# Nine raw weight buffers, x times rstd on GpSimd chunk by chunk, the modulated x in PSUM, spills on ScalarE's queue and residual x fetched ahead, in a one-core hybrid RG-LRU / pooling block

## The chip, the cores and the metric

The kernel runs on one core of one Trainium2 chip. The metric is the device time of one execution in microseconds (us); the times given are medians of repeated runs on the chip. The engines are called PE (TensorE; PEld are its weight loads), DVE (VectorE), ACT (ScalarE), POOL (GpSimd) and SP (SyncE, which here only issues DMAs).

## The reference, cut to what matters

256 latent and 256 context tokens of width 4096 pass one mixer layer, all in fp32:

```python
mod = silu(c) @ w_ada + b_ada                 # shift, scale, gate: 3 x 4096
h  = rmsnorm(x, g_norm) * (1 + scale) + shift
xa, xb, ga, gb = split(h @ w_in)              # 4 x 4096
xa_c = (modulated rmsnorm(ctx)) @ w_in[:, :4096]
ya = rglru_branch(xa, xa_c, ...)              # conv, two gates per head and direction, scans
yb = pool_branch(xb, w_pool, ...)             # windows 2, 4, 8, 16
mixed = concat(ya * silu(ga), yb * silu(gb))
out = rmsnorm(x + gate * (mixed @ w_out), g_final)
```

Shift, scale and gate come from the weights `w_ada` (a product with one vector for the latent and one for the context tokens), so `w_ada` is read in full, as `w_in` and `w_out` are.

## The kernel before

Everything is held transposed: a tile has 128 features as partitions and the 512 tokens (latent, then context) along the free dimension. fp32 products are made from splits: each operand is `hi`, rounded to fp32r, plus the rest `lo`. A unit of weights is a 128x1024 tile of 512 KB that SP loads into a buffer `raw` (pool of RAWB = 6); ACT casts it to `hi` (pool of 4, L97) and `lo = raw - hi` is made (pool of 3, L99), by POOL for the xa projection and by DVE elsewhere.

The stages:

- **Start.** x and ctx (32 tiles) come in, their squares are summed over the features (L402, L403) and L412 sums over partitions; `rstd_of` (L160) makes the reciprocal root. Meanwhile PE makes the first chunk's shift and scale rows from `w_ss` units (L237). `to_cols` and `finish_mod` (L202 to L204) turn rows into the columns `colA`, `colB`.
- **xa.** The 32 feature tiles of h are dealt in nine chunks of 2, 2, 4, 4, ... tiles (CHUNKS). `prep_h(k)` multiplies x tile k by rstd (L300, on DVE), applies colA and colB (L303, on ACT, in place) and splits the result into `hhi` and `hlo` (L130, L131). `xa_units(c)` then multiplies chunk c with its part of `w_in`, three matmuls to a product (L337 to L339), and adds the partial sum into 32 accumulators: three of four output tiles through ACT and POOL (L345, L346), the fourth on DVE (L348). Beside chunk c the shift and scale of chunk c + 1 are made out of `w_ss` units: a few on PE (L237; SHARES says how many), most on DVE, as multiply-adds into two PSUM tiles (L211 to L219). `softplus` (L358), a chain of some 25 small DVE operations on the scan's decay, stands after chunk 1.
- **Mixer.** The latent projections and pooling products (two matmuls to a product, L566 with 512 and L567 with 256 columns), beside them the recurrent heads.
- **Output.** `make_mix` splits the gated branches; 16 blocks of two output tiles, 16 units each, are multiplied with `w_out`. Beside them DVE sums three groups of `w_gate` units (L213; the first group came earlier). `out_evac` folds a tile, multiplies by gate, adds the residual x, squares it for the final norm and, for the first ten blocks, spills y to DRAM.
- **End.** The spilled tiles are read back, the final norm's rstd is made, and y is scaled and stored.

The order is written by `run(events)`: events of kind "w" (a weight unit that is split) and "a" (a raw unit that is used as it is) are loaded LOOK = 4 and LOOK_A = 2 events of their kind ahead; "s" events are other work. `spread` deals side work evenly among main work. All buffers of `raw` serve both kinds and are handed out in the order of the loads. A scheduler then fixes the order of each engine at build time, taking an instruction that its model finds ready before an earlier one that it finds waiting. All DMAs are issued by SP, in order. PSUM holds four tiles of 512 columns (`mm_tile`) and two of 1024 (`wide_tile`).

Of the kernel before, what the change touches and what calls it, by code (L numbers as in the profile page):

```python
# [7 lines left out]
F32 = mybir.dt.float32  # L8
F32R = mybir.dt.float32r
AF = mybir.ActivationFunctionType  # L10
ALU = mybir.AluOpType
ADD, SUB, MUL = ALU.add, ALU.subtract, ALU.mult

P = 128
D = 4096
KT = D // P
T = 256
# [4 lines left out]
GATE3 = (0.08, 0.7)  # L22
GATE_FROM, GATE_END = 0.9, 0.99
SPILL_Y = 10
EPS = 1e-6
POOL_ADDS = 3
EARLY = 4
NPREP = 3
LAGS = (0, 2, 5, 7, 10)
LRU_SPAN = 91  # L30
RAWB, HIB, LOB = 6, 4, 3
LOOK = 4
LOOK_A = 2
X_STEP = 3
SHARES = (16, 4, 11, 3, 0, 0, 0, 0, 0, 0, 0, 0)
CHUNKS = (2, 2, 4, 4, 4, 4, 4, 4, 4)
# [10 lines left out]


def spread(main, side, lo=0.0, hi=1.0):
    """Places the entries of side evenly among those of main, from the fraction lo of main to hi."""  # L50
    out, done, n = [], 0, len(main)
    a, b = lo * n, hi * n
    for i, m in enumerate(main):
        out.append(m)
        want = min(len(side), max(0, int((i + 1 - a) / (b - a) * len(side) + 1e-9)))
        while done < want:
            out.append(side[done])
            done += 1
    return out + side[done:]
# [3 lines left out]
def block_kernel(ctx, tc, xc, cvec, vecs, consts, w_ss, w_gate, w_xa, w_lat, w_pool, w_rec, w_out, out):  # L63
# [16 lines left out]
    def temp(name, dt=F32):  # L80
        return tpool.tile([P, 512], dt, name=name, tag="t")

    def mm_tile():
        return ps_mm.tile([P, 512], F32, name="mm", tag="mm")
# [9 lines left out]
    def load_w(src, eng=None):  # L94
        raw = load_raw(src)
        hi = hip.tile([P, W], F32R, name="hi", tag="hi")
        act.copy(out=hi, in_=raw)  # L97
        lo = lop.tile([P, W], F32R, name="lo", tag="lo")
        (eng or dve).tensor_tensor(out=lo, in0=raw, in1=hi.bitcast(F32), op=SUB)  # L99
        return hi, lo  # L100

    def run(events):
        queues = {}
# [22 lines left out]
    def S_(f):  # L126
        return ("s", f)

    def split(hi, lo, src):
        act.copy(out=hi, in_=src)  # L130
        dve.tensor_tensor(out=lo, in0=src, in1=hi.bitcast(F32), op=SUB)  # L131

# [1 line left out]
    cst = cpool.tile([P, 276], F32, name="cst")  # L134
    nc.sync.dma_start(out=cst, in_=consts)
    ident = cst[:, 0:4]
# [20 lines left out]
    dve.tensor_tensor(out=sc6[:, :, 2:4], in0=sc, in1=sig, op=MUL)  # L157
    act.activation(out=sig, in_=sig, func=AF.Sqrt)

    def rstd_of(ps, r, v, s):  # L160
        """Leaves -2 * rsqrt(ps / D + EPS) in r: one Newton step after the square root."""
        dve.tensor_scalar(out=v, in0=ps, scalar1=1.0 / D, scalar2=EPS, op0=MUL, op1=ADD)
        act.activation(out=s, in_=v, func=AF.Sqrt)
        dve.reciprocal(out=r, in_=s)
        dve.tensor_tensor(out=v, in0=v, in1=r, op=MUL)
        dve.tensor_tensor(out=v, in0=v, in1=r, op=MUL)
        dve.scalar_tensor_tensor(out=r, in0=v, scalar=-3.0, in1=r, op0=ADD, op1=MUL)

# [1 line left out]
    colA = cpool.tile([P, KT, 2], F32, name="colA")  # L170
    colB = cpool.tile([P, KT, 2], F32, name="colB")
    gate = cpool.tile([P, KT], F32, name="gate")
# [116 lines left out]
            to_cols(st["rb"], 2, 512, dst)  # L289
        return [unit(k) for k in range(KT)], S_(rows), S_(cols)  # L290

# [1 line left out]
    hT = [None] * KT  # L293
    hc = [None] * KT

    def prep_h(k):
        def f():
            x = xt[k]
            if k >= CHUNKS[0]:
                dve.tensor_tensor(out=x, in0=x, in1=rstd, op=MUL)  # L300
            for v in range(2):
                xs = x[:, v * T:(v + 1) * T]
                act.activation(out=xs, in_=xs, func=AF.Identity, scale=colA[:, k, v:v + 1], bias=colB[:, k, v:v + 1])  # L303
            hi, lo = temp("hhi", F32R), temp("hlo", F32R)
            split(hi, lo, x)
            hc[k] = (hi, lo)
        return S_(f)

# [7 lines left out]
            hc[k] = None  # L316
        return S_(f)

# [1 line left out]
    acc = [None] * 32  # L320
    xa_sp = [None] * (2 * KEEP) + [dram.tile([P, 512], F32, name=f"xa_sp{o}") for o in range(2 * KEEP, 32)]
    ya_sp = [dram.tile([P, 512], F32, name=f"ya_sp{h}") for h in range(HEADS)]
# [1 line left out]
    def xa_units(c):  # L324
        k0, n = chunk_kt[c]
        per = W // n // P

        def unit(i):
            def f(w):
                hi, lo = (t.rearrange("p (k m) -> p k m", k=n) for t in w)  # L330
                for j in range(per):
                    o = i * per + j
                    ps = mm_tile()
                    for k in range(n):
                        a, b = hc[k0 + k]
                        wh, wl = hi[:, k, j * P:(j + 1) * P], lo[:, k, j * P:(j + 1) * P]
                        pe.matmul(out=ps, lhsT=wh, rhs=a, start=(k == 0), stop=False)  # L337
                        pe.matmul(out=ps, lhsT=wh, rhs=b, start=False, stop=False)  # L338
                        pe.matmul(out=ps, lhsT=wl, rhs=a, start=False, stop=(k == n - 1))  # L339
                    if c == 0:  # L340
                        acc[o] = slot("acc")
                        act.copy(out=acc[o], in_=ps)
                    elif c < NC - 1 and o % 4 < POOL_ADDS:
                        part = temp("part")
                        act.copy(out=part, in_=ps)  # L345
                        nc.gpsimd.tensor_tensor(out=acc[o], in0=acc[o], in1=part, op=ADD)  # L346
                    else:
                        dve.tensor_tensor(out=acc[o], in0=ps, in1=acc[o], op=ADD)  # L348
                    if c == NC - 1 and o >= 2 * KEEP:
                        nc.sync.dma_start(out=xa_sp[o], in_=acc[o])  # L350
                        acc[o] = None
            return W_(w_xa[xa_base[c] + i], f, nc.gpsimd)
        return [unit(i) for i in range(32 // per)]
# [25 lines left out]

    ada = [ada_units(c) for c in range(NC)] + [([],)]  # L380

# [1 line left out]
    xt = []  # L383
    first = ada[0][0] + list(ada[0][1:])

# [25 lines left out]
    stat = mm_tile()  # L411
    pe.matmul(out=stat, lhsT=ones, rhs=ssq, start=True, stop=True)  # L412
    rstd = slot("rstd")
    rstd_of(stat, rstd, temp("v"), temp("s"))
    for k in range(CHUNKS[0]):
        dve.tensor_tensor(out=xt[k], in0=xt[k], in1=rstd, op=MUL)
    while first:
        first_unit()
    events = [prep_h(k) for k in range(CHUNKS[0])]
# [1 line left out]
    for c in range(NC):  # L421
        main = xa_units(c)
        if c + 1 < NC:
            k1, n1 = chunk_kt[c + 1]
            preps = [prep_h(k) for k in range(k1, k1 + n1)]
            au, ar, ac = ada[c + 1]
            au = au[early:]
            nxt = ada[c + 2][0]
            cut = len(nxt) // EARLY
            lag = [nxt[cut * LAGS[i] // 10:cut * LAGS[i + 1] // 10] for i in range(4)]  # L430
            keeps = [keep_h(k) for k in range(chunk_kt[c][0], k1)]
            events += spread(main, au + lag[0] + [ar] + lag[1] + [ac] + lag[2] + preps[:NPREP] + lag[3]) + keeps + preps[NPREP:]
            early = cut
        else:
            events += main + [keep_h(k) for k in range(chunk_kt[c][0], KT)]
        if c == 1:
            events.append(S_(softplus))

# [1 line left out]
    def lru_pieces(h):  # L440
        st = {}

# [94 lines left out]
            return [sigm(d, 0), sigm(d, 1), expo(d), root(d), scan(d, 0), scan(d, 1)]  # L537
        return [conv(0), conv(1)], [gates(0)] + post(0) + [gates(1)], post(1)

# [1 line left out]
    def fold(ps, dst):  # L541
        tmp = temp("fold")
        act.copy(out=tmp[:, 0:T], in_=ps[:, T:T2])
# [122 lines left out]
    both = spread(both, gu, GATE_FROM, GATE_END)  # L666
    events += both[:-4] + [gr] + both[-4:-1] + [gc] + both[-1:]

# [1 line left out]
    mix = [None] * 64  # L670

    def make_mix(n):
# [12 lines left out]
    def out_evac(blk):  # L685
        def f(j, ps):
            ct = 2 * blk + j
            if j == 0:
                xr = temp("xr")
                nc.sync.dma_start(out=xr.rearrange("p (k t) -> p k t", k=2),  # L690
                                  in_=xc[ct:ct + 2, :, 0:T].rearrange("k p t -> p k t"))
                ys.append(xr)
            y = ys[blk][:, j * T:(j + 1) * T]
            v = temp("ov")[:, 0:T]
            fold(ps, v)
            dve.scalar_tensor_tensor(out=y, in0=v, scalar=gate[:, ct:ct + 1], in1=y, op0=MUL, op1=ADD)
            if ct == 0:
                sums["s"] = temp("ssum")[:, 0:T]
                act.activation(out=sums["s"], in_=y, func=AF.Square)
            else:  # L700
                act.activation(out=v, in_=y, func=AF.Square)
                if ct < 30:
                    dve.tensor_tensor(out=sums["s"], in0=sums["s"], in1=v, op=ADD)
                else:
                    sums[ct] = v
            act.activation(out=y, in_=y, func=AF.Identity, scale=gf[:, ct:ct + 1])
            if j == 1 and blk < SPILL_Y:
                nc.sync.dma_start(out=y_sp[blk], in_=ys[blk])
        return f

    def warm_sqrt():
        t = temp("warm")[:, 0:1]
        act.activation(out=t, in_=ones[:, 0:1], func=AF.Sqrt)

    events += [make_mix(n) for n in range(4)] + [S_(warm_sqrt)]
    main = [block_units([w_out[blk, i] for i in range(16)], mix, out_evac(blk)) for blk in range(16)]
    pair = [u for two in zip(main[0], main[1]) for u in two]
    main = spread(pair, [make_mix(n) for n in range(4, 32)], 0.0, 28 / 32) + [u for m in main[2:] for u in m]
    side, held = [], []
# [14 lines left out]
    for i, part in enumerate((sums["s"], sums[30], sums[31])):  # L734
        pe.matmul(out=stat[:, 0:T], lhsT=ones, rhs=part, start=(i == 0), stop=(i == 2))
    rf = temp("rf")[:, 0:T]
    rstd_of(stat[:, 0:T], rf, temp("v")[:, 0:T], temp("s")[:, 0:T])
    for blk in range(16):
        y = ys[blk].rearrange("p (k t) -> p k t", k=2)
        dve.tensor_tensor(out=y, in0=y, in1=rf.unsqueeze(1).broadcast_to([P, 2, T]), op=MUL)  # L740
# [76 lines left out]
```

## Time and profile before

| | |
|---|---|
| median of 3 runs | 2993.46 us (2992.93 to 2996.02) |
| profiled execution, first to last instruction | 2998.8 us, 5.3 us above the median; no other time is given for this execution |
| mean granted PE clock | 0.991 |
| busy | PE 97%, PEld 80%, DVE 75%, ACT 52%, POOL 18% |
| read from and written to HBM | 661.6 MB and 15.2 MB, 226 GB/s over the span |

The busy time of an engine is the time covered by its instructions. Matmuls overlap in the records (one begins before the one ahead of it has ended), and one that waits for its operands between two others can be hidden in that overlap, so what PE loses in a stretch is read from the count of its instructions there and their pitch at full pace, and not from its busy share alone. The rows of the trace name an instruction by its line, engine, operation and tiles; in square brackets or behind a bar is how long its engine sat idle before it and what ended the wait. A line can be that of a helper: L99 is every `lo`, L91 every load into `raw`.

### The profile page before, as it was taken

What the parts mean: (1) busy time and instruction counts of PE and PEld (TensorE: products, weight loads), DVE (VectorE), ACT (ScalarE), POOL (GpSimd) and SP (SyncE); (2) the same over time, 40 slices, a digit from 0 to 9 for tenths busy, and PEclk for the clock granted to TensorE, in tenths of its full rate; (3) what the DMA queues carried; (4) which work ended last, traced back from release to release, by engine and by line L of the source; (5) the groups of instructions that cost most, each with busy time, mean ns of one, the idle gap of its engine ahead of it and who ended that gap; (6) DMA issues with size and microseconds to landing.
All of it is one profiled execution on the core that took longest, in us unless ns stands there. A gap on an engine that the chain in (4) does not pass through costs nothing.

```text
span 2998.8 us, 40342 instructions
## 1 busy us (share of the span) xinstructions
PE 2909.6 (97%) x14992; PEld 2405.3 (80%) x14992; DVE 2256.7 (75%) x2661; ACT 1559.9 (52%) x2112; POOL 530.7 (18%) x304
## 2 busy tenths in 40 slices
PE   5999999999999999999999999999999999999997
PEld 2656777778788888888888888888888888878886
DVE  6999999998447788888777777778888766665444
ACT  4442344434436666677666666666464443333442
POOL 1466777777520000000000000000000000000000
PEclk9999999999999999999999999999999999999998
DMA  8777787887365555565665566667978888786665
GB/s 301 279 261 252 262 263 261 272 277 250 126 183 176 176 177 175 179 183 172 186 185 181 185 188 189 196 195 251 326 232 318 318 288 286 264 279 216 193 191 171
DMA packets 201142, 679.47 MB, mean 227 GB/s; under 512 B 22000, under 2 KB 30320, under 8 KB 200944
## 3 DMA queue, kind: packets, MB, share of 16 engines
q1 hardware_dynamic: 200944, 676.89, 68.9%
q8 instruction: 117, 1.92, 0.3%
q14 instruction: 81, 0.66, 0.1%
HBM read 661.60 MB, written 15.20 MB: 226 GB/s over the span
## 4 chain that ended last, share of the span: by engine, by line
PE 84%; DVE 6%; DMA 6%; issue 1%; POOL 1%; ACT 1%; SPq 0%; DVEq 0%; POOLq 0%; ACTq 0%
PE mm L566 38%; PE mm L567 19%; PE mm L337 6%; PE mm L338 6%; PE mm L339 6%; DMA raw<-in_w_gate 4%; DVE wide L213 3%; PE wide L478 2%; PE wide L480 2%; PE wide L479 2%; PE mm L237 2%; DMA raw<-in_w_ss 1%; DMA x<-in_xc 1%; DVE lo L99 1%; DVE hlo L131 1%
## 5 line engine op out<-in xcount | busy, mean ns | idle before, releaser
L97 ACT CAST hi<-raw 128x1024 fp32r<-128x1024 f32 x832 | 871.9, 1049 | 968.6 <-PE mm L566 576.3
L99 DVE TENSOR_TENSOR lo<-raw,hi 128x1024 fp32r<-128x1024 f32 x704 | 856.5, 1221 | 371.5 <-PE mm L567 282.7
L566 PE MATMUL mm<-hT,hi 128*128 128x512 f32 x3072 | 1086.8, 399 | 0.0
L567 PE MATMUL mm<-hT,lo 128*128 128x256 f32 x3072 | 862.7, 281 | 0.0
L213 DVE SCALAR_TENSOR_TENSOR wide<-raw,sc,wide 128x1024 f32<-128x1024 f32 (+1 forms) x556 | 662.4, 1240 | 153.5 <-DMA raw<-in_w_gate 119.6
L566 PE MATMUL mm<-mix,hi 128*128 128x512 f32 x2048 | 724.7, 398 | 0.0
L566 PEld LDWEIGHTS mm<-hT,hi 128*128 128x128 f32 x3072 | 577.2, 188 | 144.5 <-ACT mix L130 0.9
L567 PE MATMUL mm<-mix,lo 128*128 128x256 f32 x2048 | 577.4, 282 | 15.3 <-DVE lo L99 15.1
L567 PEld LDWEIGHTS mm<-hT,lo 128*128 128x128 f32 x3072 | 580.2, 189 | 1.3
L566 PEld LDWEIGHTS mm<-mix,hi 128*128 128x128 f32 x2048 | 386.0, 188 | 95.1 <-ACT hi L97 1.7
L337 PE MATMUL mm<-hhi,hi 128*128 128x512 f32 x1024 | 404.1, 396 | 13.1 <-ACT hhi L130 10.7
L338 PE MATMUL mm<-hlo,hi 128*128 128x512 f32 x1024 | 402.1, 393 | 9.0 <-DVE hlo L131 9.0
L567 PEld LDWEIGHTS mm<-mix,lo 128*128 128x128 f32 x2048 | 388.2, 190 | 20.8 <-DVE lo L99 20.5
L339 PE MATMUL mm<-hhi,lo 128*128 128x512 f32 x1024 | 401.0, 392 | 0.0
L99 POOL TENSOR_TENSOR lo<-raw,hi 128x1024 fp32r<-128x1024 f32 x128 | 310.6, 2427 | 207.5 <-PE mm L339 87.8
L337 PEld LDWEIGHTS mm<-hhi,hi 128*128 128x128 f32 x1024 | 193.4, 189 | 73.0 <-ACT hhi L130 11.8
L346 POOL TENSOR_TENSOR acc<-acc,part 128x512 f32<-128x512 f32 x168 | 221.7, 1331 | 116.8 <-ACT part L345 115.8
L338 PEld LDWEIGHTS mm<-hlo,hi 128*128 128x128 f32 x1024 | 193.6, 189 | 53.3 <-DVE hlo L131 13.4
L339 PEld LDWEIGHTS mm<-hhi,lo 128*128 128x128 f32 x1024 | 193.6, 189 | 42.2 <-issue 1.7
L345 ACT COPY part<-mm 128x512 f32<-128x512 f32 x168 | 97.3, 584 | 155.4 <-PE mm L339 155.0
L348 DVE TENSOR_TENSOR acc<-mm,acc 128x512 f32<-128x512 f32 x88 | 60.1, 685 | 56.6 <-PE mm L339 56.5
L478 PE MATMUL wide<-uhi,hi 128*128 128x512 f32 x256 | 100.5, 393 | 0.0
(134 smaller groups left out, 2203.0 us busy)
## 6 DMA issues: line engine op xcount, KB each, us to landing
raw<-in_w_lat SPq DMA_DIRECT2D x384, 512.0 KB, 3.7
raw<-in_w_ss SPq DMA_DIRECT2D x256, 512.0 KB, 4.6
raw<-in_w_out SPq DMA_DIRECT2D x256, 512.0 KB, 4.6
raw<-in_w_xa SPq DMA_DIRECT2D x128, 512.0 KB, 4.4
raw<-in_w_gate SPq DMA_DIRECT2D x128, 512.0 KB, 4.8
raw<-in_w_rec SPq DMA_DIRECT2D x32, 512.0 KB, 3.6
raw<-in_w_pool SPq DMA_DIRECT2D x32, 512.0 KB, 3.7
x<-in_xc SPq DMA_DIRECT2D x32, 256.0 KB, 6.6
```

Of the source, the lines that this page charges most:

```text
L97: act.copy(out=hi, in_=raw)
L99: (eng or dve).tensor_tensor(out=lo, in0=raw, in1=hi.bitcast(F32), op=SUB)
L213: dve.scalar_tensor_tensor(out=accs[v][:, :width], in0=seg, scalar=s, in1=accs[v][:, :width], op0=MUL, op1=ADD)
L337: pe.matmul(out=ps, lhsT=wh, rhs=a, start=(k == 0), stop=False)
L338: pe.matmul(out=ps, lhsT=wh, rhs=b, start=False, stop=False)
L339: pe.matmul(out=ps, lhsT=wl, rhs=a, start=False, stop=(k == n - 1))
L345: act.copy(out=part, in_=ps)
L346: nc.gpsimd.tensor_tensor(out=acc[o], in0=acc[o], in1=part, op=ADD)
L348: dve.tensor_tensor(out=acc[o], in0=ps, in1=acc[o], op=ADD)
L478: pe.matmul(out=o, lhsT=wh[:, g, k, m], rhs=st["hi"][k], start=(k == 0), stop=False)
L566: pe.matmul(out=ps, lhsT=hi[:, k, m], rhs=a, start=first, stop=False)
L567: pe.matmul(out=ps[:, 0:T], lhsT=lo[:, k, m], rhs=a[:, 0:T], start=False, stop=last)
```

## The change

- RAWB from 6 to 9, LOOK from 4 to 5, LOOK_A from 2 to 4. The memory comes from a smaller scratch area for dynamic DMAs (1024).
- x by rstd moves from DVE (L300) to GpSimd, and is held in GpSimd's order behind the `lo` of the last weight unit used so far (`issue_after`). The first chunk's two tiles stay on DVE.
- `rstd_of` works in place in PSUM with one temporary in SBUF; the first chunk is multiplied by the PSUM copy, and ACT copies it to the tile `rstd`.
- The modulated x (L303's output) goes into a PSUM tile from `mm_tile`; `hhi` and `hlo` are split from there.
- `softplus` stands after chunk 7 in place of chunk 1.
- y is spilled by a DMA that ACT issues. The residual x of a block is fetched by an event of its own ahead of the block's unit 12, and no more at the block's end.

```diff
-RAWB, HIB, LOB = 6, 4, 3
-LOOK = 4
-LOOK_A = 2
+RAWB, HIB, LOB = 9, 4, 3
+LOOK = 5
+LOOK_A = 4
...
-    def rstd_of(ps, r, v, s):
-        """Leaves -2 * rsqrt(ps / D + EPS) in r: one Newton step after the square root."""
-        dve.tensor_scalar(out=v, in0=ps, scalar1=1.0 / D, scalar2=EPS, op0=MUL, op1=ADD)
-        act.activation(out=s, in_=v, func=AF.Sqrt)
-        dve.reciprocal(out=r, in_=s)
-        dve.tensor_tensor(out=v, in0=v, in1=r, op=MUL)
-        dve.tensor_tensor(out=v, in0=v, in1=r, op=MUL)
-        dve.scalar_tensor_tensor(out=r, in0=v, scalar=-3.0, in1=r, op0=ADD, op1=MUL)
+    def rstd_of(ps, r):
+        w = temp("rw")[:, 0:ps.shape[-1]]
+        dve.tensor_scalar(out=ps, in0=ps, scalar1=1.0 / D, scalar2=EPS, op0=MUL, op1=ADD)
+        act.activation(out=w, in_=ps, func=AF.Sqrt)
+        dve.reciprocal(out=w, in_=w)
+        dve.tensor_tensor(out=ps, in0=ps, in1=w, op=MUL)
+        dve.tensor_tensor(out=ps, in0=ps, in1=w, op=MUL)
+        dve.scalar_tensor_tensor(out=r, in0=ps, scalar=-3.0, in1=w, op0=ADD, op1=MUL)
...
             if k >= CHUNKS[0]:
-                dve.tensor_tensor(out=x, in0=x, in1=rstd, op=MUL)
+                with tc.issue_after(lo_ins[used[0] - 1].ins):
+                    nc.gpsimd.tensor_tensor(out=x, in0=x, in1=rstd, op=MUL)
+            h = mm_tile()
             for v in range(2):
-                xs = x[:, v * T:(v + 1) * T]
-                act.activation(out=xs, in_=xs, func=AF.Identity, scale=colA[:, k, v:v + 1], bias=colB[:, k, v:v + 1])
+                cut = slice(v * T, (v + 1) * T)
+                act.activation(out=h[:, cut], in_=x[:, cut], func=AF.Identity, scale=colA[:, k, v:v + 1],
+                               bias=colB[:, k, v:v + 1])
             hi, lo = temp("hhi", F32R), temp("hlo", F32R)
-            split(hi, lo, x)
+            split(hi, lo, h)
...
-    rstd_of(stat, rstd, temp("v"), temp("s"))
+    rstd_of(stat, stat)
     for k in range(CHUNKS[0]):
-        dve.tensor_tensor(out=xt[k], in0=xt[k], in1=rstd, op=MUL)
+        dve.tensor_tensor(out=xt[k], in0=xt[k], in1=stat, op=MUL)
+    act.copy(out=rstd, in_=stat)
...
-        if c == 1:
+        if c == NC - 2:
             events.append(S_(softplus))
...
-            if j == 0:
-                xr = temp("xr")
-                nc.sync.dma_start(out=xr.rearrange("p (k t) -> p k t", k=2),
-                                  in_=xc[ct:ct + 2, :, 0:T].rearrange("k p t -> p k t"))
-                ys.append(xr)
...
             if j == 1 and blk < SPILL_Y:
-                nc.sync.dma_start(out=y_sp[blk], in_=ys[blk])
+                act.dma_start(out=y_sp[blk], in_=ys[blk])
...
+    def fetch_x(blk):
+        def f():
+            xr = temp("xr")
+            nc.sync.dma_start(out=xr.rearrange("p (k t) -> p k t", k=2),
+                              in_=xc[2 * blk:2 * blk + 2, :, 0:T].rearrange("k p t -> p k t"))
+            ys.append(xr)
+        return S_(f)
...
+    for blk in range(16):
+        main[blk].insert(FETCH_X, fetch_x(blk))
...
-    nc = bacc.Bacc("TRN2", target_bir_lowering=False, num_devices=1)
+    nc = bacc.Bacc("TRN2", target_bir_lowering=False, num_devices=1, dynamic_dma_scratch_size=1024)
```

## Rows read from the trace of the kernel before

**Rows 1.** The page's head.

```profile
span 2998.8 us, 40342 instructions
```

**Rows 2.** Timeline, 40 to 66 us: start, length, engine, line, tiles, count, idle before.

```profile
43.68 10.52 PE L237 MATMUL mm<-raw,sc 128*4 128x256 f32 x48
...
50.81 3.46 DVE L416 TENSOR_TENSOR x<-x,rstd 128x512 f32<-128x512 f32 x2
...
54.19 8.59 DVE L300 TENSOR_TENSOR x<-x,rstd 128x512 f32<-128x512 f32 x7
...
54.71 0.60 PE L192 MATMUL mm<-cst,rows 4*128 4x4 f32 x4 [0.51 <-ACT rows L185]
62.70 0.15 DVE L202 TENSOR_TENSOR colB<-mm,vec 128x4 f32<-128x4 f32 x1
...
65.77 0.80 PE L337 MATMUL mm<-hhi,hi 128*128 128x512 f32 x1 [10.45 <-ACT hhi L130]
```

**Rows 3.** Timeline of PE alone in chunk 4, 28 matmuls from first to last.

```profile
429.49 0.39 PE L339 MATMUL mm<-hhi,lo 128*128 128x512 f32 x1
...
435.61 0.39 PE L339 MATMUL mm<-hhi,lo 128*128 128x512 f32 x1
```

**Rows 4.** Timeline of PE alone in the last block, 24 pairs from first to last.

```profile
2965.09 0.40 PE L566 MATMUL mm<-mix,hi 128*128 128x512 f32 x1
...
2973.57 0.40 PE L566 MATMUL mm<-mix,hi 128*128 128x512 f32 x1
```

**Rows 5.** Windows: stretch, length, busy (count) of PE, PEld, DVE, ACT, POOL; clock, DMA, GB/s.

```profile
0.00:64.00 64.00, 33.59 (x134) 11.62 (x134) 41.36 (x54) 27.59 (x42) 8.73 (x9) 0.94 0.94 344
65.70:200.00 134.30, 129.52 (x488) 80.71 (x489) 124.29 (x142) 55.17 (x86) 64.67 (x36) 0.97 0.76 263
200.00:300.00 100.00, 92.21 (x371) 66.39 (x370) 93.20 (x106) 38.16 (x62) 65.16 (x39) 0.97 0.71 247
300.00:870.00 570.00, 561.24 (x2431) 448.49 (x2430) 463.91 (x438) 227.54 (x354) 392.13 (x221) 1.00 0.72 240
2228.00:2433.00 205.00, 205.00 (x1160) 176.53 (x1160) 156.72 (x172) 90.25 (x113) 0.00 (x0) 1.00 0.86 303
2433.00:2720.00 287.00, 271.70 (x1507) 231.92 (x1507) 186.05 (x185) 111.02 (x131) 0.00 (x0) 0.99 0.83 278
```

**Rows 6.** The same windows for L237 alone: PE, PEld, clock, DMA.

```profile
65.70:200.00 134.30, 33.56 (x92) 6.67 (x92) 0.97 0.76 263
200.00:300.00 100.00, 10.93 (x20) 1.49 (x20) 0.97 0.71 247
300.00:870.00 570.00, 17.98 (x40) 3.06 (x40) 1.00 0.72 240
```

**Rows 7.** Groups by line: busy us, mean ns, idle before.

```profile
L131 DVE TENSOR_TENSOR hlo<-x,hhi 128x512 fp32r<-128x512 f32 x32 | 41.8, 1308 | 6.6 <-ACT hhi L130 6.6
...
L300 DVE TENSOR_TENSOR x<-x,rstd 128x512 f32<-128x512 f32 x30 | 32.5, 1125 | 0.0
...
L348 DVE TENSOR_TENSOR acc<-mm,acc 128x512 f32<-128x512 f32 x88 | 60.1, 685 | 56.6 <-PE mm L339 56.5
...
L346 POOL TENSOR_TENSOR acc<-acc,part 128x512 f32<-128x512 f32 x168 | 221.7, 1331 | 116.8 <-ACT part L345 115.8
...
L373 DVE TENSOR_SCALAR spw<-spw 128x64 f32<-128x64 f32 x8 | 6.9, 868 | 0.0
```

**Rows 8.** Waits of PE's weight loads, 65.7 to 396 us: sum, times, longest.

```profile
PEld mm L237 <- DMA raw<-in_w_ss: 12.9, 8, 4.4
...
PEld mm L337 <- DVE acc L348: 3.2, 2, 2.3
```

**Rows 9.** Waits of all engines, 2433 to 2720 us.

```profile
DVE wide L213 <- DMA raw<-in_w_gate: 92.4, 45, 5.0
...
PE mm L567 <- DVE lo L99: 15.1, 13, 2.5
```

**Rows 10.** Waits of SP's DMA issues, 2228 to 2720 us.

```profile
SPq L708 <- ACT xr L706: 17.9, 7, 6.2
```

More of the change, by code (lines that the diff above doesn't have):

```diff
@@ L24 @@
 SPILL_Y = 10
+FETCH_X = 12
 EPS = 1e-6
@@ L98, in load_w @@
         lo = lop.tile([P, W], F32R, name="lo", tag="lo")
-        (eng or dve).tensor_tensor(out=lo, in0=raw, in1=hi.bitcast(F32), op=SUB)
+        ins = (eng or dve).tensor_tensor(out=lo, in0=raw, in1=hi.bitcast(F32), op=SUB)
+        if eng is not None:
+            lo_ins.append(ins)
         return hi, lo
+    lo_ins, used = [], [0]
     def run(events):
@@ L299, in f @@
             if k >= CHUNKS[0]:
-                dve.tensor_tensor(out=x, in0=x, in1=rstd, op=MUL)
+                with tc.issue_after(lo_ins[used[0] - 1].ins):
+                    nc.gpsimd.tensor_tensor(out=x, in0=x, in1=rstd, op=MUL)
+            h = mm_tile()
             for v in range(2):
-                xs = x[:, v * T:(v + 1) * T]
-                act.activation(out=xs, in_=xs, func=AF.Identity, scale=colA[:, k, v:v + 1], bias=colB[:, k, v:v + 1])
+                cut = slice(v * T, (v + 1) * T)
+                act.activation(out=h[:, cut], in_=x[:, cut], func=AF.Identity, scale=colA[:, k, v:v + 1],
+                               bias=colB[:, k, v:v + 1])
             hi, lo = temp("hhi", F32R), temp("hlo", F32R)
-            split(hi, lo, x)
+            split(hi, lo, h)
+            xt[k] = None
             hc[k] = (hi, lo)
@@ L329, in f @@
             def f(w):
+                used[0] += 1
                 hi, lo = (t.rearrange("p (k m) -> p k m", k=n) for t in w)
@@ L736, in block_kernel @@
     rf = temp("rf")[:, 0:T]
-    rstd_of(stat[:, 0:T], rf, temp("v")[:, 0:T], temp("s")[:, 0:T])
+    rstd_of(stat[:, 0:T], rf)
     for blk in range(16):
```

## The prediction

> **What bounds the kernel now.** I read the busy shares first: PE is the bound. So the question is where PE runs below its own pace, and I read that by counting. In chunk 4, 27 steps between matmuls of 512 columns take 6.12 us, 0.2267 us each [rows 3]; in the output stage 24 pairs take 8.48 us, 0.3533 us a pair [rows 4]. The small fp32 products L237 take 10.52 / 48 = 0.219 us with 256 columns [rows 2], and I count twice that, 0.438, with 512. A column matmul L192 is 0.60 / 4 = 0.15 us, or a little less. By the windows [rows 5], less their L237 [rows 6] and the L192 that the code puts there (12, 8 and 40):
>
> - 65.7 to 200 us: 488 - 92 - 12 = 384 xa matmuls, 87.0 us; 40 L237 of 256 columns 8.8 (chunk 1, by the code), 52 of 512 22.8, L192 1.7. Sum 120.3 of 134.3: PE loses 14.0.
> - 200 to 300: 343 matmuls 77.8, L237 8.8, L192 1.0, sum 87.6 of 100: 12.4 lost.
> - 300 to 870: 2351 matmuls 533.0, L237 17.5, L192 5.2, sum 555.7 of 570: 14.3 lost over six chunks.
> - 2228 to 2433: (1160 - 12) / 2 = 574 pairs 202.8 and 2.8 for the gate columns: nothing lost.
> - 2433 to 2720: (1507 - 12) / 2 = 747.5 pairs 264.1 and 2.8, 266.9 of 287: 20.1 lost.
>
> The mixer between 870 and 2228 us and the end of the output stage run at the pair pitch and nothing in them can be gained. Before the first xa matmul there is one more hole: PE's column matmuls end at 55.31, but DVE runs `colB` only at 62.70, because seven L300 stand ahead of it in its queue; the first xa matmul comes at 65.77 after 10.45 us of idleness [rows 2]. That makes 7.4 us. All holes together: 7.4 + 14.0 + 12.4 + 14.3 + 20.1 = 68.2 us. No other edit can pay more than that, apart from the end, which the change leaves as long as it is.
>
> **The change, part by part.**
>
> *Start.* With L300 gone from DVE, `colB` can run at 55.4. The first chunk's two L416, 3.46 us together [rows 2], now read rstd from PSUM; priced like L348, which has one PSUM input, 2 x 0.685 = 1.4 [rows 7], they end some 2 us earlier, by 52.3, and are not in the way. ACT's copy of rstd, about 0.6 us, lies under PE's L237, which end at 54.2 whatever the buffers do. I take the 7.4 in full. Bounds: 3, if ACT has casts in front of the first L303, and 8.1.
>
> *DVE in the xa stage.* It is 124.3 of 134.3 us busy in the first window and 93.2 of 100 in the second [rows 5], so there DVE and PE are close to bound together. It loses: L300, 32.5 us in all, of which about a dozen instructions lie ahead of 66 us and most of the other 20 us before 200 us [rows 7]; softplus, all between 200 and 252 us, whose eight L373 alone are 6.9 us [rows 7] and whose whole I put at twice that, 14; and in hlo (L131) 1.308 - 0.685 = 0.62 us x 32 = 20 us, since a DVE operation with one operand in PSUM, L348, takes 0.685 while two SBUF operands beside a busy POOL take 1.1 to 1.3 [rows 7]. DVE falls to some 100 of 134 and 78 of 100: it is no bound any more. An hlo that takes 2 us at the start of a chunk, where PE waits for it, goes too.
>
> *Softplus later.* It lands in chunk 8, where no shift and scale are made and DVE has little but L348; its first reader is the recurrent stage after 870. Free; with the cover gone it would cost its 14 us once.
>
> *Buffers.* PE's L237 wait 12.9 us for `w_ss` transfers up to 396 us [rows 8], because a transfer is issued only when POOL or DVE has let go of one of six buffers. Three more let it go out one or two units earlier. DMA is at 263 and 247 GB/s here and reached 344 at the start [rows 5]; 263 x 134.3 / 126 = 280 leaves room. Of the three xa losses I take back 8 of 14.0 (2 to 13), 8 of 12.4 (3 to 11: softplus and the buffers both fall here) and 5 of 14.3 (0 to 10: mostly hlo). The rest stays, as part of it is the clock (granted at 0.97 of 2.4 GHz on average in the first two, so some of the time at the lower level, 1.2 GHz [rows 5]) and part the chunk change itself.
>
> *Output stage.* DVE waits 92.4 us, 45 times, for a gate transfer, and behind the waiting L213 stand the `lo` that PE needs: PE waits 15.1 us for them in 13 places [rows 9]. A gate transfer is issued when the last one's buffer is let go, and its landing is then waited for. With four ahead and nine buffers it lands before its turn; demand is one `w_out` unit of 0.524 MB in 8 x 0.3533 = 2.83 us, 185 GB/s, and 0.55 gate units beside it (96 over 176 main events), 287 GB/s in all, which the stretch before 2433 carries without loss at 303 [rows 5]. I take back 14 of 20.1 (3 to 19).
>
> *Spills and residual.* SP waits 17.9 us over ten spills for ACT's last operation on y [rows 10], with the weight loads behind it; on ACT's queue the spill waits for nothing that ACT has not just done. Its issue there, priced at about 0.4 us as on SP, is 4 us beside 111 busy of 287 [rows 5]; behind it stand casts that have slack. The residual x comes ahead of the last units instead of beside the fold. Both are counted in the 14.
>
> *New costs.* POOL takes 30 products at 1.331 us, as L346 [rows 7], 40 us on top of 522 busy in 804 [rows 5]; x and rstd are there long before, so the product waits for nothing, and behind it stand `lo` that are made units ahead. At nothing that PE feels, at most 1.3 us for each chunk after the first, 10. Against this edit speaks the Trainium skill, GPSIMD Engine Reference, § 4.1 Engine selection: products of two tiles belong on VectorE, GpSimd being about twice as slow at them. The trace agrees on the factor, 1.331 against 0.685 [rows 7]. If the whole difference, 30 x 0.65 = 19 us, came to lie on PE's path, the sum would be 21 and the time 2972; POOL's 282 idle us of 804 in the stage [rows 5] are the cover that I take to prevent it. The PSUM tile takes one of four banks from the matmuls for two L303, the cast and hlo, some 2.5 us a tile. PE now waits 3.2 us in two places for a bank that DVE frees [rows 8]. I take 2 us for both (0 to 15).
>
> Sum: 7.4 + 8 + 8 + 5 + 14 - 2 = 40.4. The profiled execution spans 2998.8 [rows 1], which gives 2958.4; the median lies 5.3 below the span, so 2953. Worst bounds together lose 4 us, best ones gain about 61.
>
> **The rivals.**
>
> *Half of it (0.17).* One of the two big pieces stays: the transfers are late for another reason, since SP issues in order and a load ahead of it waits for its buffer, or DMA near 300 GB/s is slower to land than I think. Then 12 to 25 us are gained, 2968 to 2981. For it: in the output stage DMA is 0.83 busy. Against: 0.94 has been reached [rows 5].
>
> *Almost all of it (0.08).* PE then runs at its pitch nearly everywhere: 55 to 68 us, 2925 to 2938.
>
> *The change does not do what it says (0.05).* The loads come no earlier and the scheduler puts POOL's product late, so that the 7 us of the start are given back: 2988 to 2999.
>
> *Slower (0.08): PSUM banks.* If each of 32 preparations holds up PE for one output tile, 12 x 0.2267 = 2.7 us, that is 87 us against 42: 3038. It decides from about 1.3 us a preparation, where the gain is gone. Against it: PE waits for banks only a few times now, with DVE more loaded than it will be [rows 8].
>
> **How the numbers follow.** My forecast, 2953 with a range of its own of 2938 to 2968, has 0.62. The measurement tells 0.2%, 6 us, from no change. Faster: 0.62 + 0.17 + 0.08 = 0.87; same 0.05; slower 0.08. The range takes in the bigger gain and the half of it, 2925 to 2982.
>
> **What would show it.** `colB` right after PE's column matmuls and the first xa matmul near 58; no L300 on DVE and hlo near 0.69 us throughout; the L237 waits for `w_ss` and the L213 waits for gate transfers a fraction of what they are; xa done near 844 and PE without a wait for `lo` after 2400. Wrong would be: PE's first xa matmul of a tile waiting for a bank held by the preparation, a POOL product that delays a `lo` PE waits for, or DVE still waiting for gates with the DMA busy share above 0.9.

## The result and the profile after

| | before | after |
|---|---|---|
| median, measured together | 2994.74 us (2992.93 to 2997.39) | 2964.86 us (2961.89 to 2966.97) |
| ratio after to before | | 0.9899, 95% interval 0.9885 to 0.9913 |
| span of the profiled execution | 2998.8 us [rows 1] | 2965.2 us |

The change makes the kernel 29.9 us faster. The forecast was 2953, its own range 2938 to 2968 and the whole range 2925 to 2982: the measured time lies in both, 12 us above the forecast. The direction was right, and so was the mechanism of the start and, in the main, of the xa stage; that of the output stage was not. The profiled execution of after took 2966.97 us, 1.8 more than its span.

Four starts of matmuls cut each span into stages: the first xa matmul, the last xa matmul, and the first and last matmul of `mix` (of 512 columns).

| | to first xa | xa stage | mixer | output stage | end | span |
|---|---|---|---|---|---|---|
| before | 65.8 | 803.6 | 1354.6 | 752.0 | 22.8 | 2998.8 |
| after | 58.8 | 784.9 | 1354.8 | 743.6 | 23.1 | 2965.2 |
| gained | 7.0 | 18.7 | -0.2 | 8.4 | -0.3 | 33.6 |
| forecast | 7.4 | 19 | 0 | 14 | 0 | 40.4 |

(The forecast of the xa stage is 8 + 8 + 5 less the 2 for new costs.) Executions of one program vary: a second profile of after, in the experiments, has 784.1 us in the xa stage and 740.9 in the output stage.

**Start.** The timeline of after, 40 to 62 us, answers to [rows 2]; it shows start, length, engine, line, tiles, count and idle time before.

```profile
43.72 10.52 PE L243 MATMUL mm<-raw,sc 128*4 128x256 f32 x48
...
50.84 1.28 DVE L427 TENSOR_TENSOR x<-x,mm 128x512 f32<-128x512 f32 x2
52.16 0.59 ACT L428 COPY rstd<-mm 128x512 f32<-128x512 f32 x1 [6.94 <-DVE x L427]
...
55.69 0.16 DVE L208 TENSOR_TENSOR colB<-mm,vec 128x4 f32<-128x4 f32 x1 [3.57 <-PE mm L198]
...
58.78 0.79 PE L348 MATMUL mm<-hhi,hi 128*128 128x512 f32 x1 [3.12 <-ACT hhi L135]
```

No product by rstd stands between the column matmuls and `colB` (L208): DVE now waits for PE there, where `colB` had waited for seven products. PE's hole shrinks from 10.45 to 3.12 us. The first chunk's two products take 1.28 us, as priced (1.4).

**The xa stage.** Windows of after, then the same for the `w_ss` products (L243) alone; these answer to [rows 5, 6].

```profile
58.70:188.00 129.30, 127.35 (x488) 80.83 (x488) 114.44 (x131) 57.27 (x91) 74.18 (x46) 0.98 0.82 301
188.00:283.00 95.00, 92.88 (x375) 69.02 (x376) 81.02 (x79) 34.68 (x56) 68.12 (x41) 0.96 0.75 266
283.00:850.00 567.00, 563.14 (x2457) 451.11 (x2456) 447.83 (x461) 229.62 (x357) 410.23 (x241) 1.00 0.70 239
2400.00:2690.00 290.00, 283.21 (x1573) 242.19 (x1572) 191.52 (x188) 115.18 (x135) 0.00 (x0) 0.99 0.83 281
```

```profile
58.70:188.00 129.30, 33.07 (x92) 6.92 (x92) 0.98 0.82 301
188.00:283.00 95.00, 9.23 (x20) 1.40 (x20) 0.96 0.75 266
283.00:850.00 567.00, 17.98 (x40) 3.06 (x40) 1.00 0.70 239
```

Count by count as in the prediction, with the 34 matmuls of the mixer in the third window taken apart (6.1 us), PE loses 9.0, 6.5 and 7.0 us in the first three windows, where it had lost 14.0, 12.4 and 14.3. Back came 5.0, 5.9 and 7.3, where 8, 8 and 5 were forecast (new costs apart). The groups by line for 58.7 to 850 us answer to [rows 7]; behind the bar are busy us and the mean of one in ns.

```profile
L359 DVE TENSOR_TENSOR acc<-mm,acc 128x512 f32<-128x512 f32 x88 | 60.5, 689 | 87.6 <-PE mm L350 87.6
...
L307 POOL TENSOR_TENSOR x<-x,rstd 128x512 f32<-128x512 f32 x30 | 38.5, 1297 | 0.0
...
L136 DVE TENSOR_TENSOR hlo<-mm,hhi 128x512 fp32r<-128x512 f32 x32 | 22.1, 691 | 20.5 <-ACT hhi L135 17.8 <-ACT part L356 2.4
```

`hlo` fell from 1308 to 691 ns and now waits for ACT; DVE has 81.0 busy us of 95 in the second window where it had 93.2 of 100. In the first it is still busy for 114.4 of 129.3 us, where some 100 of 134 were forecast. PE's waits over the whole span (sum, times, longest), beside [rows 8]:

```profile
PE mm L243 <- DMA raw<-in_w_ss: 11.4, 8, 1.4
...
PE mm L579 <- DVE lo L100: 6.7, 6, 2.1
PE mm L348 <- ACT hhi L135: 4.6, 2, 3.1
PE mm L348 <- DVE acc L359: 2.3, 2, 1.6
PE mm L349 <- DVE hlo L136: 1.7, 1, 1.7
PE mm L348 <- DVE hlo L136: 1.6, 1, 1.6
```

The 11.4 us for `w_ss` lie at the start, ahead of the first xa matmul; in the stage none is left. A bank that DVE frees costs 2.3 us in two places, as before (2.4). The last line is new. L348 does not read `hlo`, so what it can be waiting for there is a PSUM bank that the preparation holds until `hlo` is made. It comes once, at the start of the last chunk (timeline of 749 to 763 us):

```profile
752.81 0.69 DVE L136 TENSOR_TENSOR hlo<-mm,hhi 128x512 fp32r<-128x512 f32 x1 [2.38 <-ACT hhi L135]
...
753.56 0.50 PE L348 MATMUL mm<-hhi,hi 128*128 128x512 f32 x1 [1.61 <-DVE hlo L136]
```

In the same chunk PE waits 1.5 us more for `hhi` and 0.8 for a bank that DVE frees, 3.9 us in all; in before's last chunk it waits 0.7.

**The output stage** did not do what was forecast. The first of its waits in 2400 to 2690 us, beside [rows 9]:

```profile
DVE wide L219 <- DMA raw<-in_w_gate: 80.3, 42, 4.7
```

DVE still waits 80.3 us, 42 times, for gate transfers (92.4, 45 times before), and PE's 6.7 us for `lo` fall in the same stretch. SP's wait for y in front of the spills, 17.9 us [rows 10], is gone. What is left of waits for y stands in front of weight loads, first after, then before:

```profile
SPq L92 <- ACT xr L713: 1.3, 4, 0.4
```

```profile
SPq L91 <- ACT xr L706: 0.9, 3, 0.3
```

### The profile page after: what moved, and what is told of

It is laid out like the page before. It is cut to its first block, busy times and chain, and to the rows that moved or that the text cites. A ratio compares the mean times of both kernels' runs of the same rounds, so it can differ in the third digit from the quotient of the medians.

```text
span 2965.2 us, 40318 instructions
## 1 busy us (share of the span) xinstructions
PE 2903.5 (98%) x14992; PEld 2405.9 (81%) x14992; DVE 2203.4 (74%) x2631; ACT 1560.9 (53%) x2113; POOL 558.1 (19%) x334
## 4 chain that ended last, share of the span: by engine, by line
PE 89%; DMA 6%; DVE 3%; ACT 1%; issue 1%; SPq 0%; DVEq 0%; ACTq 0%
PE mm L578 38%; PE mm L579 19%; PE mm L348 8%; PE mm L349 8%; PE mm L350 7%; DMA raw<-in_w_gate 5%; PE wide L490 2%; PE mm L243 2%; PE wide L492 2%; PE wide L491 2%; DVE wide L219 1%; DMA x<-in_xc 1%; PE mm L198 0%; DVE lo L100 0%; PE mm L285 0%
## 5 line engine op out<-in xcount | busy, mean ns | idle before, releaser
L348 PE MATMUL mm<-hhi,hi 128*128 128x512 f32 x1024 | 403.0, 395 | 9.2 <-ACT hhi L135 4.6
L349 PE MATMUL mm<-hlo,hi 128*128 128x512 f32 x1024 | 400.9, 392 | 1.7 <-DVE hlo L136 1.7
L348 PEld LDWEIGHTS mm<-hhi,hi 128*128 128x128 f32 x1024 | 193.2, 189 | 68.3 <-issue 9.5
L357 POOL TENSOR_TENSOR acc<-acc,part 128x512 f32<-128x512 f32 x168 | 215.0, 1295 | 71.9 <-ACT part L356 67.5
L349 PEld LDWEIGHTS mm<-hlo,hi 128*128 128x128 f32 x1024 | 193.4, 189 | 43.0 <-DVE hlo L136 3.1
L359 DVE TENSOR_TENSOR acc<-mm,acc 128x512 f32<-128x512 f32 x88 | 60.5, 689 | 87.6 <-PE mm L350 87.6
```

## The experiments

All times are medians against the kernel before, run on the same chip; there were three chips, on which before had 2995.42, 2993.87 and 2995.05 us. The stages of the profiled executions, for all of them:

| run | median us | ratio, 95% interval | to first xa | xa | output |
|---|---|---|---|---|---|
| after, second time | 2963.73 | 0.9897 (0.9883 to 0.9910) | 58.7 | 784.1 | 740.9 |
| u_buf: old buffers | 2979.32 | 0.9943 (0.9929 to 0.9957) | 58.2 | 794.2 | 749.0 |
| u_look2: old LOOK_A | 2966.08 | 0.9900 (0.9886 to 0.9915) | 58.3 | 783.9 | 741.8 |
| u_pool: product on DVE | 2976.89 | 0.9935 (0.9919 to 0.9950) | 64.9 | 790.3 | 742.8 |
| u_psum: modulated x in place | 2967.21 | 0.9908 (0.9893 to 0.9923) | 57.8 | 788.7 | 741.0 |
| u_soft: softplus early | 2972.50 | 0.9923 (0.9909 to 0.9936) | 58.7 | 793.5 | 741.2 |
| u_spill: old spills, fetch | 2961.03 | 0.9886 (0.9872 to 0.9899) | 58.0 | 781.4 | 742.3 |
| hold: gate sums held | 2949.33 | 0.9845 (0.9831 to 0.9859) | 58.9 | 783.9 | 727.3 |
| hold_spill: both | 2948.13 | 0.9847 (0.9834 to 0.9860) | 58.4 | 782.7 | 727.3 |
| b_hold: before, sums held | 2975.84 | 0.9933 (0.9920 to 0.9945) | 65.7 | 802.3 | 728.5 |

The mixer is 1354.6 to 1354.9 us in all but u_buf (1356.4), the end 22.7 to 23.3.

### The buffers, and the look-ahead of raw units

Two runs undo this part of after, the first in full, the second LOOK_A alone:

```diff
-RAWB, HIB, LOB = 9, 4, 3
-LOOK = 5
-LOOK_A = 4
+RAWB, HIB, LOB = 6, 4, 3
+LOOK = 4
+LOOK_A = 2
```

> The changed kernel with six raw buffers and the old look-ahead (4 and 2); the rest as changed. Theory: the buffers gave part of the xa stage and all that the output stage gained. The output stage's loss goes from 11 back to about 20 us, the xa stage gives back 5 to 8, the start keeps its 7: 2978 to 2982 us against 2964.9. Rival: taking work off VectorE is what freed both stages and the buffers do nothing: within 3 us of 2965.

> The changed kernel with LOOK_A 2 in place of 4 and nothing else. Theory: in the output stage the scheduler uses a gate unit as soon as its model has it landed, whatever the look-ahead is, so only the number of buffers matters: within 3 us of 2965, output loss 11 plus or minus 2 us, VectorE's waits for gate transfers about 100 us as now. Rival: the units looked ahead are what covers the transfers: output loss towards 20 us, 2972 or more.

The buffers are worth 14.5 us (2979.32 less 2964.86): 9.3 in the xa stage and 5.4 in the output stage (8.1 against after's second profile). The total was as expected, the share of the xa stage larger. LOOK_A = 4 is worth nothing that can be measured: 2966.08. And with it at 2 or at 4, DVE waits for gates about as long (86.4 us, 45 times, against 80.3, 42 times). So the step "with four ahead and nine buffers it lands before its turn" can't be right as it stands.

### What the gate sums wait for

Here are SP's gate loads and DVE's gate sums in after, from two timelines of 2640 to 2663 us, one of SP, one of DVE.

```profile
2642.46 0.33 SPq L92 DMA_DIRECT2D raw<-in_w_gate  x1
...
2644.72 0.33 SPq L92 DMA_DIRECT2D raw<-in_w_gate  x1
...
2651.55 0.33 SPq L92 DMA_DIRECT2D raw<-in_w_gate  x1
...
2657.29 0.33 SPq L92 DMA_DIRECT2D raw<-in_w_gate  x1
```

```profile
2647.68 1.29 DVE L219 SCALAR_TENSOR_TENSOR wide<-raw,sc,wide 128x1024 f32<-128x1024 f32 x1 [2.99 <-DMA raw<-in_w_gate]
...
2650.24 1.29 DVE L219 SCALAR_TENSOR_TENSOR wide<-raw,sc,wide 128x1024 f32<-128x1024 f32 x1
...
2655.97 1.29 DVE L219 SCALAR_TENSOR_TENSOR wide<-raw,sc,wide 128x1024 f32<-128x1024 f32 x1 [2.18 <-DMA raw<-in_w_gate]
...
2661.12 1.29 DVE L219 SCALAR_TENSOR_TENSOR wide<-raw,sc,wide 128x1024 f32<-128x1024 f32 x1 [1.60 <-DMA raw<-in_w_gate]
```

Paired in order, each sum starts 5.2, 5.5, 4.4 and 3.8 us after its load was issued, and each new load goes out just after an earlier sum has ended (2651.55 after 2650.24 + 1.29, 2657.29 after 2655.97 + 1.29). A gate load takes 4.8 us from issue to landing in the median. Over the sums of 2400 to 2690 us, paired backwards from the last one, the median lead is 4.6 us, and it is 4.6 in before and in u_buf and 4.7 in u_look2 as well. Whatever the pool and the look-ahead allow, the sum is placed where its transfer is only just due. That points to the order fixed at build time: it takes a gate sum as soon as its model thinks it ready, ahead of the `lo` of weight units that come first in the list of events, and the buffers then fill with weight units.

The run hold tests this. It puts each gate sum behind the `lo` of the weight unit in use (`los` collects each weight unit's `lo`, `turn` counts the units used; in hold the -1 is a constant); nothing else of after changes. The lines that fill `los` and `turn` are left out here.

```diff
+                with tc.issue_after(los[turn[0] - 1].ins):
-                accumulate(raw, 0, W, k, st["accs"], 1, 512, st["fin"], k == 0, k == KT - 1)
+                    accumulate(raw, 0, W, k, st["accs"], 1, 512, st["fin"], k == 0, k == KT - 1)
```

> The changed kernel with each gate unit's sum on VectorE ordered behind the lo of the weight unit that is in use at its place in the program; the same instructions. Theory: what is left of the output stage's loss (11 us) comes from the scheduler's taking a gate sum as soon as its model has the transfer landed, so that no look-ahead is left when the transfer is later than modelled. Held back, VectorE's waits for gate transfers fall from 80 us in 2400 to 2690 to under 20, the loss to 0 to 3 us, the time to 2954 to 2957. Rival: DMA at 280 to 300 GB/s is what is late: waits only change their place, 2963 or more.

It came to 2949.33, 15.5 us below after, and the output stage fell from 743.6 (740.9 in after's second profile) to 727.3. The window of 2400 to 2690 us, and the last gate loads and sums from timelines of SP (2640 to 2655 us) and DVE (2655 to 2672):

```profile
2400.00:2690.00 290.00, 290.00 (x1660) 250.24 (x1660) 204.23 (x197) 121.89 (x140) 0.00 (x0) 1.00 0.87 298
```

```profile
2640.17 0.33 SPq L93 DMA_DIRECT2D raw<-in_w_gate  x1
...
2645.71 0.33 SPq L93 DMA_DIRECT2D raw<-in_w_gate  x1
...
2651.26 0.33 SPq L93 DMA_DIRECT2D raw<-in_w_gate  x1
```

```profile
2658.60 1.28 DVE L223 SCALAR_TENSOR_TENSOR wide<-raw,sc,wide 128x1024 f32<-128x1024 f32 x1
2663.81 1.28 DVE L223 SCALAR_TENSOR_TENSOR wide<-raw,sc,wide 128x1024 f32<-128x1024 f32 x1
2669.36 1.40 DVE L229 SCALAR_TENSOR_TENSOR fin<-raw,sc,wide 128x512 f32<-128x512 f32 x2
```

The lead is now 18.1 to 18.4 us, no gate sum waits for its transfer, PE is busy for 290.00 of 290 us with 1660 matmuls where after had 1573, and the DMA share is higher (0.87 against 0.83), not lower: the transfers were never short of bandwidth. The expectation was too high by 5 us, because it took the stage's remaining loss as 11 us, from the pair pitch of [rows 4]; the stage became 16.3 us shorter, or 13.6 by the second profile, and the last section says why.

The same edit was made to the kernel before, with its six buffers:

> The kernel before, with six buffers and the old look-ahead, and nothing of the change, but each gate unit's sum ordered behind the lo of the weight unit in use. Theory: the order of the sums alone is what made the output stage lose: its 752 us fall to 727 to 732 and the time from 2995 to 2970 to 2976. Rival: with six buffers a gate unit that waits for its turn keeps weight units out, and the stage is no shorter than 748 us, 2990 or more.

It came to 2975.84, as expected. Its window beside the last of [rows 5]:

```profile
2433.00:2720.00 287.00, 287.00 (x1642) 247.54 (x1641) 199.84 (x194) 120.79 (x140) 0.00 (x0) 1.00 0.85 294
```

PE makes 1642 matmuls there where before made 1507, and the output stage is 23.5 us shorter (752.0 to 728.5) by order alone, within 1.2 us of hold's. So nearly the whole loss of this stage was the order's. The medians give the edit 18.0 us (2993.87 less 2975.84), so part of the 23.5 belongs to the one profiled execution of before. The median lead, paired as above, is 8.3 us here and 18.1 in hold: with the order held, buffers and look-ahead do lengthen it. How the nine buffers shorten this stage without the order (u_buf) while the lead stays at 4.6 us is not shown.

### The product by rstd on GpSimd

```diff
-                with tc.issue_after(lo_ins[used[0] - 1].ins):
-                    nc.gpsimd.tensor_tensor(out=x, in0=x, in1=rstd, op=MUL)
+                dve.tensor_tensor(out=x, in0=x, in1=rstd, op=MUL)
```

> The changed kernel with x times rstd back on VectorE, not held. Theory: the first xa matmul goes back to about 65 us (7 us), and 30 products of which most run before 200 us load VectorE again: 3 to 6 us more in the xa stage: 2975 to 2978. Rival: GpSimd, twice as slow at the product, delays the lo of the weights, so that the xa stage gets shorter by as much as the start gets longer: within 3 us of 2965.

With the product back on DVE, 12.0 us are lost, as expected: 6.1 at the start and 5.4 in the xa stage. Its timeline from 48 to 66 us has the old hole again:

```profile
51.93 9.54 DVE L306 TENSOR_TENSOR x<-x,rstd 128x512 f32<-128x512 f32 x5 [0.65 <-ACT rstd L427]
...
61.40 0.15 DVE L208 TENSOR_TENSOR colB<-mm,vec 128x4 f32<-128x4 f32 x1
...
64.93 1.22 PE L347 MATMUL mm<-hhi,hi 128*128 128x512 f32 x2 [10.11 <-ACT hhi L135]
```

### The modulated x in PSUM

```diff
-            h = mm_tile()
+            h = x
```

> The changed kernel with the modulated x written back in place in SBUF, as before; the rest as changed. Theory: hlo again has two SBUF operands beside a busy GpSimd and takes 1.0 to 1.4 us in place of 0.69, and at the start of a chunk PE waits for it: 3 to 6 us, all in the xa stage, 2968 to 2971 against 2964.9. Rival: the bank that the preparation takes from the matmuls costs what hlo gains: 2962 to 2966.

Undone, it costs 2.4 us in the median, between the two ranges, and 3.8 in the profiled xa stage. `hlo` then takes 678 ns at the least, 940 in the median and 2724 at the most; L349 waits for it in six places, 8.7 us, where after has one, 1.7 us.

```profile
L136 DVE TENSOR_TENSOR hlo<-x,hhi x32: 678/940/2724, 57.8 to 762.8; 128x512 fp32r<-128x512 f32 x32
```

```profile
PE mm L349 <- DVE hlo L136: 8.7, 6, 2.6
```

In after the line of `hlo` reads 685, 692 and 692 ns. The Trainium skill, SBUF — State Buffer, § SBUF: two separate sides, says that a DVE operation with two SBUF inputs and a GpSimd operation that reads SBUF take turns on one pair of ports, the later one blocked until the first is through. The runs agree: in this run every `hlo` above 1.1 us overlaps an instruction of POOL, those that overlap none take 678 to 693 ns, and in after, with one operand in PSUM, none takes more than 692.

The 3.8 us are a net figure. Taken from the first matmul of a chunk to the first of the next, chunks 3 to 6 take 9.4 us longer with x in place, but chunks 0 to 2 take 227.2 us where five executions of after's xa stage (after, its second profile, u_spill, hold, hold_spill) need 229.3 to 232.8. So the PSUM tile seems to have a price early in the stage; part of that difference is the clock of those executions (last section), and one profile does not settle the rest.

### Softplus later

```diff
-        if c == NC - 2:
+        if c == 1:
```

> The changed kernel with softplus back after chunk 1. Theory: VectorE is 81 of 95 us busy there now, so its 14 us fill it but no longer bind PE: 0 to 3 us, 2965 to 2968. Rival, as the prediction had it: softplus is half of what the stretch between 200 and 300 us gained: 3 to 6 us, 2968 to 2971.

Both were too low: it costs 7.6 us in the median, 8.6 in the xa stage. The window of 188 to 283 us, and PE's largest wait in the stage:

```profile
188.00:283.00 95.00, 85.97 (x330) 62.82 (x331) 91.68 (x97) 30.16 (x48) 59.39 (x36) 0.93 0.69 241
```

```profile
PE mm L348 <- DVE acc L359: 8.8, 3, 4.0
```

DVE is 91.7 of 95 us busy, PE makes 330 matmuls where after makes 375, and its granted clock is 0.93 on average where after has 0.96, so more of the window lies at the lower level. The chain itself also runs slower there: in this run the two groups of eight at L383 and L384 take 838 and 1050 ns each, in after, late in the stage, 496 and 192. Undone alone, with the nine buffers and the product on POOL in place, this edit is worth a quarter of the gain.

### The spills and the residual x

```diff
-                act.dma_start(out=y_sp[blk], in_=ys[blk])
+                nc.sync.dma_start(out=y_sp[blk], in_=ys[blk])
...
+            if j == 0:
+                fetch_x(blk)[1]()
...
-    for blk in range(16):
-        main[blk].insert(FETCH_X, fetch_x(blk))
```

> The changed kernel with the spills of y on SP's queue and the residual x fetched at the block's end, as before. The output stage gained 8.4 us with the change (from its first to its last matmul) and lost 5.4 of them when the buffers were undone. Theory: the spills and fetches are the other 3: 2967 to 2969, output stage 746 to 747 us. Rival: they are worth nothing with nine buffers, 2963 to 2966.

It came out 3.9 us lower than after, below both ranges, and its profile puts 3.5 of that in the xa stage, where PE, DVE and POOL run the same instructions in the same order. The window of 188 to 283 us of this run and of after run a second time:

```profile
188.00:283.00 95.00, 93.30 (x391) 69.92 (x391) 83.82 (x81) 36.73 (x59) 69.07 (x42) 1.00 0.77 273
```

```profile
188.00:283.00 95.00, 93.31 (x379) 69.34 (x379) 81.47 (x78) 34.38 (x55) 67.79 (x41) 0.96 0.76 266
```

This execution had the full clock in that window, 1.00 against 0.96, and made 391 matmuls against 379 and 375. Two more runs were to say if the edit has a part in that: after once more, and hold with this edit on top.

> The kernel after, unchanged, to see how far its median moves from one chip and hour to the next. If the spread is as small as the runs of one call show: 2962 to 2968. If the 3.9 us below it that undoing the spills gave is such a spread: a median at or below 2963, and an xa stage below 783 us.

> The kernel after, with each gate sum held behind the lo of the weight unit in use (as in the run that held the sums) and in addition the spills put back on SP's queue and the residual x fetched at the block's end. Theory (the spills and the fetch give nothing, and the 3.9 us by which undoing them alone came out lower was the spread of single runs): 2947 to 2953, within 3 us of the run that held the sums (2949.3). Rival (undoing them gains by itself): 2944 to 2946. Second rival (the spills on ACT's queue are worth their 3 us once nothing else makes DVE wait): 2953 to 2956, with PE waits in the output stage after SP's wait for y.

After came to 2963.73 with an xa stage of 784.1, in the range of the small spread, so it did not repeat the 3.9 us. Hold with the old spills and fetch came to 2948.13, 1.2 us from hold and with the same output stage to 0.1 us. SP's waits in front of the spills, first in that run, then in b_hold with its six buffers:

```profile
SPq L722 <- ACT xr L720: 25.0, 7, 8.9
```

```profile
SPq L713 <- ACT xr L711: 17.7, 7, 4.7
```

The waits are back, and the output stages are 727.3 and 728.5 us all the same. So the spills and the fetch are worth nothing that can be measured. The 3.9 us of u_spill look like spread between executions: 3.5 of them lie in the xa stage, which is over before an edited instruction runs, and the five executions of that stage took 781.4 to 784.9 us. Medians of four runs don't prove it.

## Why the prediction was right, and where it was off

- **Start, 7.4 us: right.** 7.0 measured, 6.1 lost again with the product alone put back.
- **The xa stage, 19 us net: right in sum, with the shares off.** 18.7 measured, and the stage is done at 843.7 us where 844 was forecast. With 3.5 us between executions of this stage and the shares off, an agreement to 0.3 us is partly luck. Undoing one part at a time costs 9.3 for the buffers, 8.6 for softplus, 5.4 for the product and 3.8 for PSUM in this stage, 27.1 in all: each also covers for the others. Softplus was put at 14 us of DVE, and its instructions take 14.5 in before; at its new place it is nearly "free" (a wait of PE of 0.8 us is there and is gone in u_soft). The new costs, taken at 2 us, did show: in the last chunk PE waits 1.6 us for a bank held by the preparation, one of the prediction's signs of being wrong, and 1.5 us for `hhi`. It comes once and not at each of 32 preparations, so the rival of the PSUM banks (3038) is out. No wait of PE names POOL's products.
- **GpSimd.** The row of L307, 1297 ns against 689 for a DVE operation of the same shape (L359), has the factor of about two that the Trainium skill, GPSIMD Engine Reference, § 4.1 Engine selection, gives for operations with two inputs. Its 38.5 us lay under POOL's idle time, as taken, as far as PE's waits show.
- **Output stage, 14 us: the step that failed.** 8.4 measured (11.1 in the second profile). "A gate transfer is issued when the last one's buffer is let go, and its landing is then waited for" was a right reading of [rows 9]. "With four ahead and nine buffers it lands before its turn" was wrong: the turn moved forward too. LOOK_A did nothing, the lead stayed at 4.6 us, and only a change of order raised it. The rival "half of it" named the right symptom, but neither of its causes was what had to change: in hold SP waits for buffers longer than in after (170.3 us for `lo` against 93.8 in 2400 to 2690) and DMA moves 298 GB/s, both with no loss.
- **Spills and residual, "counted in the 14": worth nothing that can be measured.** SP's 17.9 us went, but nothing that PE needs stood behind them: hold_spill and b_hold have such waits with nine and with six buffers and lose nothing by them. With six buffers and the sums not held, u_buf and before differ by 3.0 us in this stage (749.0, 752.0), hardly more than the two profiles of after (2.7).
- **From the span to the median, 5.3 us: off.** Of the 12 us by which the forecast was too low, 6.8 are the sum (40.4 against 33.6, 5.6 of it the output stage) and 5.1 this term. Taking after's 1.8 us beside the span for both, the profiled execution of before took some 3000.6 us, 5.9 above the median of 2994.74 measured with after; after's execution is 2.1 above its own. Some of the losses that I counted in before's trace were that execution's own, so they were counted both as gain and as offset. The run b_hold, whose profiled execution is the one at its median, points to the output stage: the other stages of the two differ by 1.3 us at most, while the output stage differs by 23.5 and the medians by 18.0. In 2433 to 2720 us before's mean granted clock is 0.99 [rows 5] and b_hold's 1.00. With one profile of each this is argued, not shown.

The best version is hold, with or without the old spills: 2949.33 and 2948.13 us, 1.5% below before and about half a per cent below after.

## What to carry to other kernels

Before pricing deeper look-ahead, measure the lead that a load now has: the time from its issue to its use. If the lead is about the landing time in every place, something eager (here an order fixed by a model of the transfer) may be using the data as soon as it lands; then more buffers did not lengthen it here (4.6 us with six and with nine). Hold the consumer back behind the work that it should not overtake. Where one engine is busy nearly all of a stretch, moving a chain of tiny operations out of it can be worth about as much as three buffers (in this xa stage 8.6 us against 9.3).

## What was not expected of the hardware

**Two paces of the same pair of matmuls.** In hold, PE's pairs run without a wait at two constant paces. The first and last rows of two timelines of PE, from 2600 and from 2300 us:

```profile
2599.66 0.40 PE L583 MATMUL mm<-mix,hi 128*128 128x512 f32 x1
...
2609.03 0.39 PE L583 MATMUL mm<-mix,hi 128*128 128x512 f32 x1
```

```profile
2299.95 0.28 PE L584 MATMUL mm<-mix,lo 128*128 128x256 f32 x1
...
2309.14 0.28 PE L584 MATMUL mm<-mix,lo 128*128 128x256 f32 x1
```

That is 27 steps in 9.37 us, 0.347 us a pair, and 26 steps in 9.19 us, 0.353, at a granted clock of 1.00. The same instructions keep one pace for tens of us; the traces of before and after show both values too, and the pace changes near the gate's column matmuls or after a wait. What sets it was not found. It is why a pitch taken from one place [rows 4] hid some 5 us of the output stage's loss.

**The clock is a term between executions.** The same instructions in the same order made 375, 379 and 391 matmuls in the window of 188 to 283 us, at mean granted clocks of 0.96, 0.96 and 1.00. At 0.2267 us each, 16 matmuls are 3.6 us, about the size of the smaller edits. A part of that is u_spill's earlier start (58.0 against 58.8 us): between the same two matmuls of the xa stage, the 385th and the 577th, the three executions took 52.5, 52.3 and 49.8 us, at mean granted clocks of 0.93, 0.93 and 1.00.
